# Second MLP projection, columns 1024 to 1535: the moving weights read in another order of columns

## The chip, the cores and the metric

One core of a Trainium2 chip runs the whole program. The metric is device time in microseconds (us). For the kernel before there are three runs: 1775.53, 1778.53 and 1780.2 us, median 1778.53. One further execution was profiled. PE is TensorE, DVE is VectorE, ACT is ScalarE, POOL is GpSimd, and SP issues the large transfers.

## The reference

One layer of a decoder trunk over 256 positions of width 2048. Three branches (gated delta rule, gated linear recurrence, attention into a memory of 256 tokens) are mixed and projected. The part that the change touches is the MLP at the end:

```python
h2 = rmsnorm(x, g_pre_mlp[l])
m = jnp.square(jax.nn.relu(h2 @ w_mlp_in[l])) @ w_mlp_out[l]
x = x + rmsnorm(m, g_post_mlp[l])
```

`w_mlp_in` is 2048 x 8192, `w_mlp_out` 8192 x 2048, all in float32.

## The kernel before, in words

Every large product is done with float32 operands that are split in two: a rounded part (names ending in `h`, made by a cast on ACT) and the rest (names ending in `l`, made by a subtraction on DVE). A product is then three matmuls: activation-high by weight-high, activation-high by weight-low, activation-low by weight-high. The operands have the type `fp32r`, 4 bytes an element. In `T.matmul(out, a, b)` the second argument is the stationary operand, 128 columns that are loaded into the array, and the third is the moving operand, whose columns stream through it. The trace writes the moving operand first: `mm<-oh,mh` moves the weights `oh` over the stationary activation `mh`.

The MLP works in eight steps `e` over the 8192 hidden channels, 1024 at a time. `mlp_in(e)` (lines 1483 to 1513) makes the hidden activation of a step and `mlp_out(e)` (line 1639) adds its share of the second projection. The loop at the end runs `mlp_in(e)` and then `mlp_out(e - 1)`, and `mlp_out_last` does the last step, so `mlp_out` is called for e from 0 to 6. The 2048 output columns are four blocks `c` of 512. Blocks 0 and 1 go through seven block products with sums of weights (`seven`, lines 1542 to 1598), which accumulate in `accs`. Blocks 2 and 3 go straight through `unit` (line 232), with the seven products laid around them: `part(0)` before the unit, `part(1)` in its middle, after its second group of weights.

A call of `unit` here has eight slices of 128 hidden channels, in four groups of two. For each slice and each of the two halves `t` of the positions it issues the three matmuls of lines 256 to 258, each with 512 moving columns: 8 x 2 x 3 = 48 matmuls. They accumulate in two PSUM banks `mm`, one for each half. Behind the unit, one addition for each half on DVE (line 1653) adds the bank to `yacc[c][t]`, 128 x 512 in SBUF; for e = 0 a copy on ACT writes it instead.

The weights of a group come by one DMA from HBM into one of six `raw` buffers (`raw`, line 1452), are cast into `oh` and subtracted into `ol` (`split_w`, line 216), with six pairs of `oh` and `ol` in a ring. A row of `wh[:, j, :]` is 512 elements that lie one behind the other in each partition. PSUM banks named `mm` come from a ring of four (`pbp`) and of two pairs (`pmm`). Nothing in the change alters a queue or the order in which instructions are issued.

Three older steps serve as measures in what follows. Line 1220, on ACT, reads every fourth, every 16th and every 64th element of the tile `bm` (under the name `PP`; its step is 4 x s elements with s = 1, 4, 16) and writes the exponential to `qp`; line 1218 (`seg(0, s)` from `bv(PP, s)`) reads every second element of the same tile when s = 1. Line 475, on DVE, sums the identity matrix `ident`, 128 elements a partition, with a step of 16 elements, into `dblk`. Line 969, also on DVE, sums `tm`, 128 elements that lie one behind the other, into `xc`.

Of the kernel before, what the change touches and what calls it, by code (L numbers as in the profile page):

```python
# [14 lines left out]
ALU = mybir.AluOpType  # L15
# [25 lines left out]
def tile_trunk(ctx: ExitStack, tc, a):  # L41
# [22 lines left out]
    V, A, T = Placed(nc.vector), Placed(nc.scalar), Placed(nc.tensor)  # L64
# [25 lines left out]
    def nm(s):  # L90
        cnt[0] += 1
        return f"{s}_{cnt[0]}"

    def g4(name, shape=(P, 1024), dt=F32):
        return gp.tile(list(shape), dt, tag="g", name=nm(name))
# [11 lines left out]
    def bank(name):  # L107
        return pbp.tile([P, 512], F32, tag="bp", name=nm(name))

    def const(name, shape, dt=F32):  # L110
        return cst.tile(list(shape), dt, tag=name, name=name)
# [76 lines left out]
    def tick(share=1.0):  # L188
        credit[0] += rate[0] * share
        n = int(credit[0])  # L190
        credit[0] -= n
        pump(n)
# [36 lines left out]
    def load_w(src, k0, n, c0, width=512, home=None, aside=False):  # L229
        return split_w(load_w_raw(src, k0, n, c0, width), n, width, home=home, aside=aside)  # L230

    def unit(act, nk, src, c0, r0=0, order=None, split=False, post=None, ws=None, load=None):

        if split:
            ps = [bank("mm") for _ in range(2)]
        else:
            both = pmm.tile([P, 1024], F32, tag="mm", name=nm("mm"))  # L240
            ps = [both[:, 0:512], both[:, 512:1024]]
        if order is None:
            order = [(g, None) for g in range(nk // KG)]
        ws = ws or {}
        for i, (g, tt) in enumerate(order):
            k0 = g * KG
            if g not in ws:
                ws[g] = load(src, r0 + k0, c0) if load else load_w(src, r0 + k0, KG, c0)
            wh, wl = ws[g]
            for j in range(KG):  # L250
                kt = k0 + j
                ah, al = act(kt)
                for t in range(NT) if tt is None else (tt,):
                    o = ps[t]
                    st, sl = ah[:, t * P:(t + 1) * P], al[:, t * P:(t + 1) * P]
                    T.matmul(o, st, wh[:, j, :], start=kt == 0, stop=False)
                    T.matmul(o, st, wl[:, j, :], start=False, stop=False)
                    T.matmul(o, sl, wh[:, j, :], start=False, stop=kt == nk - 1)
            tick()
            if post is not None and i + 1 in post:  # L260
                post[i + 1](ps)
        return ps if split else both
# [34 lines left out]
    def unit_joined(both_of, src, c0):  # L297


        out = g4("sum", (P, 4, S))  # L300
        tiles, ps, ws = [], [], {}
        for i, (gs, h, turned) in enumerate(halved):
            if i in (0, 1):
                tiles.append(pmm.tile([P, 1024], F32, tag="mm", name=nm("mm")))
                ps.extend((tiles[-1][:, 0:512], tiles[-1][:, 512:1024]))
            for g in gs:
                if g not in ws:
                    ws[g] = load_w(src, g * KG, KG, c0, aside=True)
            groups = [(g * KG, ws[g], [flat(both_of(kt)) for kt in range(g * KG, g * KG + KG)]) for g in gs]
            for _ in products_joined(ps, groups, KT, range(4) if h is None else (2 * h, 2 * h + 1), turned):  # L310
                tick(0.5 if h is None else 0.25)
            if 7 in gs:
                o = out[:, 2 * h:2 * h + 2, :]
                p = tiles[h].rearrange("p (c s n) -> p c s n", c=2, s=2)
                A.copy(o, p[:, :, 1, :])
                V.tensor_tensor(out=o, in0=p[:, :, 0, :], in1=o, op=ALU.add)
        return out

    def act_of(tiles):
        return lambda kt: (tiles[kt // 4][0][:, kt % 4, :], tiles[kt // 4][1][:, kt % 4, :])  # L320
# [309 lines left out]
    for u in range(2):  # L630
        ps = unit(mem_act, KT, w_kv, 1024 + 512 * u) if u else first_unit(w_kv, 1024)
        if u == 0:
            bg.append(gen_start())
            pump(1)
        pair = (g4("cvh", (P, NT, 512), F32R), g4("cvl", (P, NT, 512), F32R))
        for t in range(NT):
            split_scaled([(ps[:, t * 512:(t + 1) * 512], pair[0][:, t, :], pair[1][:, t, :], rsm[:, t:t + 1])])
        Vt.append(pair)
# [447 lines left out]
    for hg in range(2):  # L1086
        kc = conv(unit_joined(hboth, w_in, OFF_AK + 512 * hg), 1, hg)
        qc = conv(unit_joined(hboth, w_in, OFF_AQ + 512 * hg), 0, hg)
        vc = conv(unit_joined(hboth, w_in, OFF_AV + 512 * hg), 2, hg)
        z = z_evac(unit(hact, KT, w_in, OFF_AZ + 512 * hg), gna)  # L1090
        bg.append(gen_a(hg, kc, qc, vc, z))
# [213 lines left out]
    for hg in range(2):  # L1305
        k, g = forget(unit_joined(hboth, w_in, OFF_BF + 512 * hg), hg)
        q = unit_joined(hboth, w_in, OFF_BQ + 512 * hg)
        own_table(A.activation(q, q, AF.Silu))
        ps = unit(hact, KT, w_in, OFF_BI + 512 * hg)
# [31 lines left out]
    st = const("sty", [P, 8])  # L1341
# [24 lines left out]
    def mix_last(ps, t):  # L1366
        mix_square(3, t, ps[t])
        v, ry = small("vy", 1), small("ry", 1)
        V.tensor_scalar(out=v, in0=st[:, t * 4 + 3:t * 4 + 4], scalar1=1.0 / D, scalar2=stm[:, t:t + 1],
                        op0=ALU.mult, op1=ALU.add)  # L1370
        G.tensor_tensor(out=ry, in0=v, in1=mhalf[:, 0:1], op=ALU.pow)
        for c in range(4):
            if c == 2:
                mix_gain(3, t, ps[t])
            V.scalar_tensor_tensor(out=xs[c][:, t, :], in0=ys[c][:, t, :], scalar=ry, in1=xs[c][:, t, :],
                                   op0=ALU.mult, op1=ALU.add)
            pt = bank("tr")
            for k in range(4):
                T.transpose(pt[:, k * P:(k + 1) * P], xs[c][:, t, k * P:(k + 1) * P], ident)
            split_scaled([(pt[:, k * P:(k + 1) * P], h2T[c][0][:, k, t * P:(t + 1) * P],  # L1380
                           h2T[c][1][:, k, t * P:(t + 1) * P], gcol[:, 32 + c * 4 + k:33 + c * 4 + k]) for k in range(4)])
# [8 lines left out]
    for c in range(4):  # L1390
        ys.append(g4("y1", (P, NT, 512)))
        if c < 3:
            ps = unit(mact, KT, a["w_out"][0], 512 * c)
# [6 lines left out]
        else:  # L1400
# [3 lines left out]
            ps = unit(mact, KT, a["w_out"][0], 512 * c, order=last, split=True,  # L1404
                      post={8: first_weights, 11: lambda ps: mix_last(ps, 0)})
# [60 lines left out]
    w_mo = a["w_mlp_out"][0]  # L1466
# [142 lines left out]
    yacc = [None] * 4  # L1609
# [25 lines left out]
    def load_xs(c):  # L1635
        xs[c] = g4("x2", (P, NT, 512))
        nc.sync.dma_start(xs[c], xd[c])

    def mlp_out(e, mt, ops, after):
        summed, bare = seven(e, mt, ops)  # L1640
        for c, part in ((2, summed), (3, bare)):
            if c == 3 and after is not None:
                bg.append(after)
            part(0)
            ps = unit(act_of(mt), 8, w_mo, c * 512, e * 8, split=True, load=load_in, post={2: lambda ps: part(1)})
            if e == 0:
                y_ = g4("yacc", (P, NT, 512))
                yacc[c] = [y_[:, t, :] for t in range(NT)]
            for t in range(NT):
                if e == 0:  # L1650
                    A.copy(yacc[c][t], ps[t])
                else:
                    V.tensor_tensor(out=yacc[c][t], in0=ps[t], in1=yacc[c][t], op=ALU.add)

    def mlp_out_last(e, mt):
        yacc[0:2] = joined()
# [23 lines left out]
    for e in range(1, NE):  # L1680
        cur, rs = mlp_in(e)
        drain()
        if e == NE - 1:
            gbc = load_gbc(a["g_post_mlp"])
        later = []
        mlp_out(e - 1, prev, ops, gen_sums(rs, later) if e < NE - 1 else None)
        prev, ops = cur, later
# [15 lines left out]
```

## Time and profile before

| what | value |
|---|---|
| median of three runs | 1778.53 us |
| the profiled execution's own time | 1777.77 us |
| its span, first to last instruction | 1776.0 us |
| mean granted TensorE clock | 0.999 |
| PE busy | 1761.3 us, 99% |
| DVE busy | 1303.4 us, 73% |
| ACT busy | 961.8 us, 54% |
| matmul instructions on the chip | 9053 |
| additions into `yacc` on DVE | 28, mean 688 ns |

The span is 1.8 us shorter than the execution's own time, and the own time 0.8 us below the median. Busy time of matmuls is a union: a matmul's record is longer than the distance to the next one, because they overlap in the array. The rate at which PE works is therefore read from the distance between two starts.

### The profile page before, as it was taken

The page shows a single profiled execution, that of the slowest core. Times are in us where ns is not written, and L with a number is a line of the kernel's source. Part 1 is how long each engine was busy: PE and PEld are TensorE (multiplying, and loading weights), DVE is VectorE, ACT ScalarE, POOL GpSimd, SP SyncE. Part 2 cuts the span into 40 slices and gives each one's busy share as a digit, 9 for nine tenths or more (in the row PEclk, how much of TensorE's full clock was granted, in tenths as well). Part 3 has the DMA queues.
Part 4 walks back from the last instruction along what each step waited for, and adds up shares of the span by engine and source line. Part 5 has one row for each costly group of instructions (what it writes and reads, how often), then busy time and mean ns, then how long its engine had stood idle before and what let it go on. Part 6 is the DMA issues. An engine that isn't in the chain of part 4 may idle for free.

```text
span 1776.0 us, 23962 instructions
## 1 busy us (share of the span) xinstructions
PE 1761.3 (99%) x9053; PEld 1495.8 (84%) x9053; DVE 1303.4 (73%) x1764; ACT 961.8 (54%) x1217; POOL 58.0 (3%) x100
## 2 busy tenths in 40 slices
PE   9999999999999999999999999999999999999998
PEld 7888888888888888888888888888888888888886
DVE  6765768685859487698555557796979797969796
ACT  6644666454555475565444445665545464646453
POOL 1000000400030000000000000000000000000000
PEclk9999999999999999999999999999999999999999
DMA  8665555875587465555666665767767676767683
GB/s 265 214 193 166 168 160 165 220 216 159 161 216 210 135 190 166 158 174 168 188 189 189 235 222 198 233 228 237 229 226 249 220 250 214 257 204 250 212 295 144
DMA packets 188804, 362.84 MB, mean 204 GB/s; under 512 B 14456, under 2 KB 16272, under 8 KB 188304
## 3 DMA queue, kind: packets, MB, share of 16 engines
q1 hardware_dynamic: 181856, 351.32, 62.2%
q0 software_dynamic: 2304, 5.44, 1.5%
q10 hardware_dynamic: 4528, 4.54, 0.9%
q8 instruction: 71, 1.16, 0.3%
q14 instruction: 45, 0.37, 0.1%
HBM read 356.86 MB, written 4.39 MB: 203 GB/s over the span
## 4 chain that ended last, share of the span: by engine, by line
PE 77%; DVE 5%; issue 2%; DMA 1%; ACT 1%; DVEq 0%; POOLq 0%; POOL 0%; ACTq 0%
PE mm L56 73%; DVE ol L56 3%; PE pa L56 1%; DMA raw<-in_w_mlp_out 1%; DVE relu L56 1%; DVE raw L56 1%; PE kk L56 0%; DVE ml L56 0%; PE bo L56 0%; PE o L56 0%; PE pzt L56 0%; PE pw L56 0%; PE tr L56 0%; PE y L56 0%; PE oT L56 0%
## 5 line engine op out<-in xcount | busy, mean ns | idle before, releaser
L56 DVE TENSOR_TENSOR wl<-w,wh 128x1024 fp32r<-128x1024 f32 (+1 forms) x362 | 436.7, 1217 | 234.9 <-ACT wh L56 212.7
L56 ACT CAST wh<-w 128x1024 fp32r<-128x1024 f32 (+1 forms) x362 | 375.5, 1047 | 354.6 <-PE mm L56 293.2
L56 ACT CAST oh<-raw 128x1024 fp32r<-128x1024 f32 x288 | 299.3, 1053 | 274.8 <-PE mm L56 195.8
L56 DVE TENSOR_TENSOR ol<-raw,oh 128x1024 fp32r<-128x1024 f32 x288 | 343.2, 1221 | 95.5 <-ACT oh L56 65.3
L56 PE MATMUL mm<-wh,hh 128*128 128x512 f32 x1152 | 366.2, 392 | 0.0
L56 PEld LDWEIGHTS mm<-wh,hh 128*128 128x128 f32 x1152 | 216.1, 188 | 44.6 <-ACT wh L56 0.3
L56 PE MATMUL mm<-wl,hh 128*128 128x512 f32 x576 | 224.5, 390 | 0.0
L56 PE MATMUL mm<-h2h,oh 128*128 128x512 f32 x960 | 224.3, 390 | 0.0
L56 PEld LDWEIGHTS mm<-h2h,oh 128*128 128x128 f32 x960 | 178.1, 188 | 35.8
L56 PE MATMUL mm<-hh,wh 128*128 128x512 f32 x768 | 184.6, 391 | 0.8 <-ACT z L56 0.8
L56 PEld LDWEIGHTS mm<-hh,wh 128*128 128x128 f32 x768 | 140.6, 188 | 28.3 <-ACT z L56 1.0
L56 PE MATMUL mm<-ol,mh 128*128 128x512 f32 x372 | 145.3, 391 | 1.6 <-DVE ol L56 1.6
L56 PE MATMUL mm<-oh,mh 128*128 128x512 f32 x372 | 145.4, 391 | 0.0
L56 PE MATMUL mm<-oh,ml 128*128 128x512 f32 x372 | 143.8, 389 | 0.0
L56 PEld LDWEIGHTS mm<-wl,hh 128*128 128x128 f32 x576 | 108.2, 188 | 21.2
L56 PEld LDWEIGHTS mm<-h2h,ol 128*128 128x128 f32 x960 | 117.4, 189 | 3.0 <-DVE ol L56 0.7
L56 PE MATMUL mm<-h2h,ol 128*128 128x256 f32 x960 | 118.5, 281 | 0.5 <-DVE ol L56 0.5
L56 PEld LDWEIGHTS mm<-hh,wl 128*128 128x128 f32 x768 | 97.1, 188 | 3.4
L56 PE MATMUL mm<-hh,wl 128*128 128x256 f32 x768 | 99.7, 280 | 0.0
L56 PEld LDWEIGHTS mm<-ol,mh 128*128 128x128 f32 x372 | 69.8, 188 | 17.8 <-DVE ol L56 3.7
L56 PEld LDWEIGHTS mm<-oh,mh 128*128 128x128 f32 x372 | 69.8, 188 | 16.1 <-DVE acc L56 1.6
L56 PEld LDWEIGHTS mm<-oh,ml 128*128 128x128 f32 x372 | 69.8, 188 | 14.4
(363 smaller groups left out, 2208.7 us busy)
## 6 DMA issues: line engine op xcount, KB each, us to landing
w<-in_w_in SPq DMA_DIRECT2D x240, 512.0 KB, 4.2
raw<-in_w_mlp_out SPq DMA_DIRECT2D x170, 512.0 KB, 4.6
raw<-in_w_mlp_in SPq DMA_DIRECT2D x118, 512.0 KB, 4.8
w<-in_w_out SPq DMA_DIRECT2D x32, 512.0 KB, 4.2
w<-in_w_kv_mem SPq DMA_DIRECT2D x30, 512.0 KB, 5.0
w<-in_w_br_c SPq DMA_DIRECT2D x16, 512.0 KB, 3.6
w<-in_w_br_a SPq DMA_DIRECT2D x16, 512.0 KB, 4.3
w<-in_w_br_b SPq DMA_DIRECT2D x16, 512.0 KB, 3.6
```

What stands on the lines that cost most here:

```text
L56: ins = op(*args, **kwargs)
```

## The change

A table `turns` gives each `e` a pair (b, q). In block 2 the 512 columns of a slice of weights are seen as b runs, in each of which the elements are read with a step of q: first the elements 0, q, 2q and so on of the run, then 1, q + 1 and so on. All three matmuls of a slice read their moving operand that way. The columns of the two PSUM banks then stand in this other order, and the addition into `yacc` writes (and reads) `yacc` with the same pattern, which puts them right. The bank itself is read straight through. For e = 0 the pair is (1, 1), and for block 3 too: nothing changes there.

| e | (b, q) | step between elements read one after the other | elements in one sweep |
|---|---|---|---|
| 1 | (1, 2) | 2 elements, 8 bytes | 256 |
| 2 | (1, 16) | 16 elements, 64 bytes | 32 |
| 3 | (1, 64) | 64 elements, 256 bytes | 8 |
| 4 | (32, 2) | 2 elements, 8 bytes | 8, in runs of 16 |
| 5 | (1, 4) | 4 elements, 16 bytes | 128 |
| 6 | (8, 4) | 4 elements, 16 bytes | 16, in runs of 64 |

```diff
-    def unit(act, nk, src, c0, r0=0, order=None, split=False, post=None, ws=None, load=None):
+    def unit(act, nk, src, c0, r0=0, order=None, split=False, post=None, ws=None, load=None, way=lambda x_: x_):
...
-                    T.matmul(o, st, wh[:, j, :], start=kt == 0, stop=False)
-                    T.matmul(o, st, wl[:, j, :], start=False, stop=False)
-                    T.matmul(o, sl, wh[:, j, :], start=False, stop=kt == nk - 1)
+                    T.matmul(o, st, way(wh[:, j, :]), start=kt == 0, stop=False)
+                    T.matmul(o, st, way(wl[:, j, :]), start=False, stop=False)
+                    T.matmul(o, sl, way(wh[:, j, :]), start=False, stop=kt == nk - 1)
...
+    turns = [(1, 1), (1, 2), (1, 16), (1, 64), (32, 2), (1, 4), (8, 4)]
+
     def mlp_out(e, mt, ops, after):
...
-            ps = unit(act_of(mt), 8, w_mo, c * 512, e * 8, split=True, load=load_in, post={2: lambda ps: part(1)})
+            b, q = turns[e] if c == 2 else (1, 1)
+            ps = unit(act_of(mt), 8, w_mo, c * 512, e * 8, split=True, load=load_in, post={2: lambda ps: part(1)},
+                      way=lambda x_: x_.rearrange("p (b a q) -> p b q a", b=b, q=q))
...
-                    V.tensor_tensor(out=yacc[c][t], in0=ps[t], in1=yacc[c][t], op=ALU.add)
+                    y_ = yacc[c][t].rearrange("p (b a q) -> p b q a", b=b, q=q)
+                    V.tensor_tensor(out=y_, in0=ps[t].rearrange("p (b q a) -> p b q a", b=b, q=q), in1=y_, op=ALU.add)
```

Every engine has as many instructions as before, in the same places. The only rows that read otherwise are the twelve additions of the six slices on DVE. Here they are for e = 2, with their neighbours:

```order
 L56 TENSOR_TENSOR ol_9710<-raw_9703,oh_9709 128x1024
 L56 TENSOR_TENSOR relu_11187<-relu_11187 128x4x128
-L56 TENSOR_TENSOR yacc_10422<-mm_11566,yacc_10422 128x512
-L56 TENSOR_TENSOR yacc_10422<-mm_11567,yacc_10422 128x512
+L56 TENSOR_TENSOR yacc_10422<-mm_11566,yacc_10422 128x16x32
+L56 TENSOR_TENSOR yacc_10422<-mm_11567,yacc_10422 128x16x32
 L56 TENSOR_TENSOR ol_9712<-raw_1690_9704,oh_9711 128x1024
 L56 TENSOR_TENSOR relu_11187<-relu_11187,relu_11355 128x4x128
```

The addition has the same 512 elements in 16 sweeps of 32; nothing stands elsewhere than before.

## The prediction

> **What bounds the kernel now.** I read the page's table of busy time first, then the waits of PE, then the sequence in time around one of the changed slices.
>
> ```profile
> PE 1761.3 (99%) x9053; PEld 1495.8 (84%) x9053; DVE 1303.4 (73%) x1764; ACT 961.8 (54%) x1217; POOL 58.0 (3%) x100
> PE mm L56 <- DVE ol L56: 3.2, 7, 1.1
> PE mm L56 <- DVE ol L56: 1.6, 5, 0.6
> ```
>
> The second row is from PE's waits over the whole span, the third from the same view for 1250 to 1700 us, where the first five changed slices lie. PE is busy for all but 14.7 us of the span, and in that stretch it waits five times for a subtraction on DVE, 1.6 us together. So whatever lengthens or shortens a matmul there moves the end by as much, except for those 1.6 us.
>
> The next rows are PE's sequence of instructions in time, for e = 1: start, duration, engine, line, operation.
>
> ```profile
> 1267.21 0.39 PE L56 MATMUL mm<-oh,mh 128*128 128x512 f32 x1
> 1268.22 0.50 PE L56 MATMUL mm<-ol,mh 128*128 128x512 f32 x1 [0.62 <-DVE ol L56]
> ...
> 1270.31 0.39 PE L56 MATMUL mm<-oh,mh 128*128 128x512 f32 x1
> ...
> 1275.52 0.39 PE L56 MATMUL mm<-oh,ml 128*128 128x512 f32 x1
> ```
>
> From 1270.31 to 1275.52 lie 23 distances of the second half of the changed unit (24 of its 48 matmuls): 5.21 / 23 = 0.2266 us for 512 moving columns. That is the rate, not the 0.39 of a record. The wait at 1268.22 stands between the unit's halves, in the seven products.
>
> Does the distance follow the columns? In the first projection two runs of 32 stand behind each other, one of 256 and one of 512 columns:
>
> ```profile
> 1310.26 3.93 PE L56 MATMUL mm<-h2h,ol 128*128 128x256 f32 x32
> 1314.02 7.44 PE L56 MATMUL mm<-h2h,oh 128*128 128x512 f32 x32
> 1321.30 0.87 PE L56 MATMUL mm<-h2h,ol 128*128 128x256 f32 x6
> ```
>
> 3.76 / 32 = 0.1175 us and 7.28 / 32 = 0.2275 us: 256 more columns cost 0.110 us, 0.43 ns a column. PE is bound by its columns, nearly without a fixed part.
>
> **The change: the matmuls.** It removes and adds no instruction and moves none. Six slices of 48 matmuls, 288 in all, read their moving operand with a step. Two slices (e = 1 and 4, 96 matmuls) take every second element, 8 bytes apart; four (e = 2, 3, 5, 6, 192 matmuls) take elements 16, 64 or 256 bytes apart. No matmul of the trace does that, so the price is bounded from other engines that read SBUF with a step. These are groups of ACT and of DVE by shape:
>
> ```profile
> L56 ACT ACTIVATE kp<-bR 128x1024 f32<-128x1024 f32 x4 | 4.2, 1058 | 0.4 <-DVE bR L56 0.3
> L56 ACT ACTIVATE junk<-x 128x512 f32<-128x512 f32 x16 | 9.9, 620 | 0.0
> L56 ACT ACTIVATE qp<-bm 128x256 f32<-128x256 f32 x2 | 1.3, 658 | 0.0
> L56 ACT ACTIVATE qp<-bm 128x64 f32<-128x64 f32 x2 | 0.6, 309 | 0.0
> ...
> L56 DVE TENSOR_REDUCE ss<-sq 128x8 f32<-128x1024 f32 x4 | 4.9, 1221 | 4.2 <-ACT sq L56 4.2
> L56 DVE TENSOR_REDUCE xc<-tm 128x8 f32<-128x128 f32 x4 | 1.2, 289 | 0.1
> L56 DVE TENSOR_REDUCE dblk<-ident 128x16 f32<-128x128 f32 x1 | 0.4, 368 | 0.0
> ```
>
> On ACT, elements that lie one behind the other cost (1058 - 620) / 512 = 0.855 ns each, which leaves 182 ns fixed. The 256 elements of `qp<-bm` lie 16 bytes apart, the 64 elements 64 bytes: (658 - 309) / 192 = 1.82 ns each, and (309 - 182) / 64 = 1.98 ns for the 64 alone. Hence 256 elements with a step take longer than 512 without. On DVE, neighbours cost (1221 - 289) / 896 = 1.04 ns, and `dblk<-ident`, 64 bytes apart, takes 79 ns longer than `xc<-tm` for as many elements: 1.04 + 79 / 128 = 1.66 ns. Since a step of 64 bytes costs about what one of 16 does, the unit paid for is a piece of 16 bytes, 1.66 to 1.98 ns each, whatever is used of it.
>
> What of a step of 8 bytes, two elements a piece? The first exponentials over `bm` are one of 512 elements with that step and one of 256 with a step of 16 bytes; the view of the tile's instructions, for 649 to 651 us and for 651 to 656 us, where only the latter is left:
>
> ```profile
> L56 ACT ACTIVATE qp<-bm x2: 665/667/669, 650.0 to 650.5; 128x512 f32<-128x512 f32 x1, 128x256 f32<-128x256 f32 x1
> L56 ACT ACTIVATE qp<-bm x1: 665/665/665, 650.5 to 650.5; 128x256 f32<-128x256 f32 x1
> ```
>
> So 669 ns for 512 elements in 256 pieces: (669 - 182) / 256 = 1.90 ns a piece, again the same. ACT hardly feels it, because two elements cost it 1.71 ns anyway.
>
> Now PE. Its 512 columns without a step are 128 pieces of 16 bytes in 226.6 ns: 1.77 ns a piece. That is just the price of a piece on the other two engines, between DVE's 1.66 and ACT's 1.98. I take this as PE's limit too: PE already gets its moving operand as fast as pieces come, four columns to a piece. Then a step of 8 bytes needs 256 pieces, 453 ns (+226.6), and a step of 16 bytes or more 512 pieces, 906 ns (+680).
>
> The bounds: at the low end nothing (the row of 226.6 ns, if PE fetches ahead of need); a gain is excluded, since columns, bytes and instructions are the same. At the high end ACT's dearest rows: 512 x 1.98 - 226.6 = 787 ns and 256 x 1.90 - 226.6 = 260 ns. I take 1.77 ns, as it is PE's own row and the nearest to both measures.
>
> Sum: 96 x 0.2266 = 21.8 us and 192 x 0.680 = 130.5 us, together 152.3 us; by the high end 25 + 151 = 176 us, by 1.72 ns a piece (four times the 0.43 ns a column) 21 + 127 = 148 us.
>
> [...]
>
> **The additions and the waits.** Twelve additions of `yacc` on DVE read one operand and write with the step; the eight with 16 bytes or more may be slower.
>
> ```profile
> L56 DVE TENSOR_TENSOR yacc<-mm,yacc 128x512 f32<-128x512 f32 x28 | 18.6, 688 | 6.0 <-PE mm L56 5.7
> ...
> 1262.00:1280.00 18.00, 17.38 (x75) 13.65 (x75) 17.98 (x20) 11.34 (x12) 0.00 (x0) 1.00 0.82 264
> 1258.87:1264.32 5.45, 5.45 (x26) 4.50 (x25) 5.45 (x6) 3.06 (x3) 0.00 (x0) 1.00 0.57 183
> ```
>
> The windows give length, then busy time of PE, weight loads, DVE and ACT. An addition takes 688 ns; with DVE's 0.62 ns more an element the read adds 0.32 us, and as much again if the write pays too: 0.64 us, 8 x 0.64 = 5.1 us. DVE is full from 1262 to 1280 (17.98 of 18.00), so without cover this could reach PE through the next `ol`. But in my case the cover grows: half a unit with a long step takes 24 x 0.906 = 21.7 us in place of 5.45, and DVE's work in it stays what it was. I cost the additions at nothing, and the five waits at -1.6 us, because DVE, which they are for, gets ahead during the longer unit. Transfers and casts likewise have more time; what is late next is PE itself.
>
> The end: the profiled execution took 1777.8 us (span 1776.0 and 1.8 around it), 0.8 below the median. 1777.8 + 152.3 - 1.6 = 1928.5. I say 1928; this case's own range is 148 - 1.6 to 176 - 1.6 above, 1924 to 1952.
>
> **The rivals.** *Two elements a piece are enough* (PE fetches pieces twice as fast as ACT does): 8-byte steps are free, the others halve the rate. For it: engines of different speed could have ports of different speed, and PE's 1.77 ns is only an upper bound of what a piece costs it. Against: the three prices agree within 20%. 192 x 0.2266 = 43.5, less 1.6: 1820. [...]
>
> *Any step halves the rate* (two neighbours are fetched together, otherwise one): 288 x 0.2266 = 65.3, less 1.6: 1841. For it: nothing but that 8 bytes is what two columns need. Against: 64 and 16 bytes would have to cost what 8 do, while on ACT the piece of 16 bytes decides.
>
> *Not slower: PE's reads are fetched far enough ahead.* Place: the read of the moving operand, all 288 matmuls. It decides if PE can get a new piece for every column, one each 0.43 ns, four times as fast as 1.77. Then the distance stays 0.2266, the matmuls cost nothing, and only the additions remain, 0 to 5.1 us against waits of 1.6: 1777 to 1783. For it: the trace never shows PE waiting for an operand in SBUF, and 0.43 ns a column may simply be the array's own rate. Against: ACT and DVE both pay although their columns come two to three times slower.
>
> That the change does not do what it says is no case: the additions have the new pattern, and the matmuls must have it for the sums to meet.
>
> **How the numbers follow.** My case 0.50; two a piece 0.20; any step 0.07; not slower 0.18; something else 0.05 (mixtures of steps and runs, or above 1952). A measurement here tells about 0.3%, 5.3 us, from no change. "Not slower" reaches to +5 us, so 0.03 of its 0.18 goes to slower and 0.14 to the same, 0.01 to faster. Slower: 0.50 + 0.20 + 0.07 + 0.05 + 0.03 = 0.85. The range takes in my case, any step and two a piece, from a little below 1820 (a rate halved from a slightly faster one, 192 x 0.2 = 38 less 1.6: 1814) to 1952 rounded: 1813 to 1950. It leaves out "not slower" and the tails, about 0.2.
>
> **What would show it.** Right: the distance between starts in the unit of block 2 is about 0.45 us for e = 1 and 4 and 0.9 us for e = 2, 3, 5, 6, alike for all three matmuls of a slice; block 3's units stay at 0.227; PE's waits for `ol` in 1250 to 1700 us are gone; DVE is no longer full there. Two a piece: 0.227 for e = 1 and 4. Any step: 0.45 in all six. Not slower: 0.227 everywhere. Wrong in another way: a price that grows with the step (e = 3 above e = 5), that depends on the run (e = 4 unlike e = 1, e = 6 unlike e = 5), or a granted clock that falls while PE streams slowly.

## The result, and the profile after

| | before | after |
|---|---|---|
| median of the runs | 1778.42 us | 1841.70 us (1840.77 to 1843.23, 4 runs) |
| span of the profiled execution | 1776.0 us | 1840.1 us |
| mean granted TensorE clock | 0.999 | 0.999 |

The ratio is 1.0357, with a 95% interval of 1.0344 to 1.0370. The change costs 63.3 us. Forecast were 149.5: the sign was right, the size more than twice too large. The time is inside the range, and within 1 us of the rival "any step halves the rate", so the first question is whether that rival's reason is the right one. (It is not.)

The page's busy times and PE's waits over the whole span:

```profile
PE 1826.8 (99%) x9053; PEld 1502.1 (82%) x9053; DVE 1307.2 (71%) x1764; ACT 961.9 (52%) x1217; POOL 57.8 (3%) x100
PE mm L56 <- DVE ol L56: 1.4, 2, 0.9
```

PE's busy time has grown by 65.5 us, the span by 64.1. Both remaining waits for `ol` lie outside the changed stretch: between 1250 and 1760 us the view of PE's waits is empty. The window that was full on DVE before now reads (length, then busy time of PE, weight loads, DVE, ACT):

```profile
1262.00:1280.00 18.00, 18.00 (x53) 10.27 (x52) 13.53 (x14) 7.17 (x7) 0.00 (x0) 1.00 0.63 203
```

PE is full, DVE has fallen from 17.98 to 13.53. The price itself stands in PE's sequence in time. These are the first and the last start of the 24 matmuls in the second half of the changed unit, for e = 1 to 6 in order:

```profile
1274.86 0.61 PE L56 MATMUL mm<-oh,mh 128*128 128x512 f32 x1
1285.27 0.63 PE L56 MATMUL mm<-oh,ml 128*128 128x512 f32 x1
...
1370.38 0.59 PE L56 MATMUL mm<-oh,mh 128*128 128x512 f32 x1
1380.33 0.61 PE L56 MATMUL mm<-oh,ml 128*128 128x512 f32 x1
...
1466.80 0.72 PE L56 MATMUL mm<-oh,mh 128*128 128x512 f32 x1
1478.06 0.67 PE L56 MATMUL mm<-oh,ml 128*128 128x512 f32 x1
...
1564.44 0.64 PE L56 MATMUL mm<-oh,mh 128*128 128x512 f32 x1
1575.46 0.66 PE L56 MATMUL mm<-oh,ml 128*128 128x512 f32 x1
...
1661.32 0.62 PE L56 MATMUL mm<-oh,mh 128*128 128x512 f32 x1
1671.88 0.64 PE L56 MATMUL mm<-oh,ml 128*128 128x512 f32 x1
...
1757.71 0.62 PE L56 MATMUL mm<-oh,mh 128*128 128x512 f32 x1
1768.27 0.64 PE L56 MATMUL mm<-oh,ml 128*128 128x512 f32 x1
```

Each difference, divided by 23, is the distance between two matmuls:

| e | step | distance, us | against 0.2266 |
|---|---|---|---|
| 1 | 8 bytes | 0.4526 | 2.00 |
| 2 | 64 bytes | 0.4326 | 1.91 |
| 3 | 256 bytes | 0.4896 | 2.16 |
| 4 | 8 bytes, runs of 16 elements | 0.4791 | 2.11 |
| 5 | 16 bytes | 0.4591 | 2.03 |
| 6 | 16 bytes, runs of 64 elements | 0.4591 | 2.03 |

The six excesses over 0.2266 add up to 1.4125 us; times 48 that is 67.8 us. PE's busy time, which holds no waits, has grown by 65.5; less the 1.6 us of waits that are gone the sum is 66.2, against 64.1 in the span. So the rate of the 288 matmuls accounts for the whole cost, to within some 2 us. Step for step: 8 bytes cost what was forecast; 16 bytes and more cost a third of what was forecast.

### The profile page after: what moved, and what is told of

Same layout as the page of the kernel before. It is cut to its first block, busy times and chain, and to the rows that moved or that the text cites. A ratio compares the mean times of both kernels' runs of the same rounds, so it can differ in the third digit from the quotient of the medians.

```text
span 1840.1 us, 23962 instructions
## 1 busy us (share of the span) xinstructions
PE 1826.8 (99%) x9053; PEld 1502.1 (82%) x9053; DVE 1307.2 (71%) x1764; ACT 961.9 (52%) x1217; POOL 57.8 (3%) x100
## 4 chain that ended last, share of the span: by engine, by line
PE 83%; DVE 1%; ACT 1%; issue 1%; DMA 0%; DVEq 0%; POOLq 0%; POOL 0%
PE mm L56 79%; PE pa L56 1%; PE kk L56 0%; DVE ol L56 0%; PE bo L56 0%; PE o L56 0%; ACT oh L56 0%; DMA raw<-in_w_mlp_out 0%; PE pzt L56 0%; PE pw L56 0%; PE tr L56 0%; DVE raw L56 0%; PE y L56 0%; PE oT L56 0%; PE mgT L56 0%
## 5 line engine op out<-in xcount | busy, mean ns | idle before, releaser
L56 PE MATMUL mm<-oh,mh 128*128 128x512 f32 x372 | 169.8, 456 | 0.0
L56 PE MATMUL mm<-ol,mh 128*128 128x512 f32 x372 | 169.1, 455 | 0.0
L56 PE MATMUL mm<-oh,ml 128*128 128x512 f32 x372 | 168.1, 455 | 0.0
```

The lines of the kernel that those rows point to most:

```text
L56: ins = op(*args, **kwargs)
```

## The experiments

After the result my own account (one piece of 16 bytes each 1.77 ns, whatever is used of it) could not stand as it was: four times as many pieces cost only twice the time (433 to 490 ns for 512, 226.6 for 128). What remained were three theories. PAIR: PE takes two columns at once where they are neighbours, otherwise one (the reason behind the rival that met the time). PIECE: a piece of 16 bytes costs a fixed time, but about half of what I took. ROW: the fast rate needs one unbroken run. Most kernels change only block 2 in the six slices, so that one execution gives six prices, each read from PE's sequence as above. The third leaves the matmuls straight, and the fourth and the last two go beyond block 2.

### Runs of neighbours kept together

```diff
-    turns = [(1, 1), (1, 2), (1, 16), (1, 64), (32, 2), (1, 4), (8, 4)]
+    turns = [(1, 1), (2, 2), (8, 2), (32, 2), (2, 4), (4, 4), (2, 16)]
...
-                      way=lambda x_: x_.rearrange("p (b a q) -> p b q a", b=b, q=q))
+                      way=lambda x_: x_.rearrange("p (a q r) -> p q a r", q=q, r=r))
```

> Six slices as in the change, but short runs of neighbours stay together: pairs of elements 16, 64 and 256 bytes apart (e = 1, 2, 3), four elements every 32 and every 64 bytes (e = 4, 5), sixteen every 128 bytes (e = 6). Theory PAIR (PE takes two columns at once where they are neighbours in 8 bytes, else one, so that any single-element step doubles a matmul): the distance between matmuls stays at 0.217 to 0.227 us in all six, time 1775 to 1782 us. Theory PIECE (a 16-byte piece costs 0.85 to 1.77 ns, the prediction's idea in a milder form): 0.45 us for e = 1 to 3, 0.227 for e = 4 to 6, 1778 + 144 x 0.226 = 1811 us. Theory ROW (the fast rate needs one run over all 512 columns): 0.45 us in all six, about 1843 us.

Measured: 1807.54 us, ratio 1.0176 (1.0160 to 1.0193). Pairs 16 and 64 bytes apart, then four neighbours every 64 bytes, first and last of 24 starts:

```profile
1273.46 0.61 PE L56 MATMUL mm<-oh,mh 128*128 128x512 f32 x1
1283.87 0.63 PE L56 MATMUL mm<-oh,ml 128*128 128x512 f32 x1
...
1368.98 0.59 PE L56 MATMUL mm<-oh,mh 128*128 128x512 f32 x1
1378.89 0.61 PE L56 MATMUL mm<-oh,ml 128*128 128x512 f32 x1
...
1643.52 0.39 PE L56 MATMUL mm<-oh,mh 128*128 128x512 f32 x1
1648.68 0.38 PE L56 MATMUL mm<-oh,ml 128*128 128x512 f32 x1
```

0.4526, 0.4309 and 0.2243 us. The pairs 256 bytes apart took 0.4896, the four neighbours every 32 bytes 0.2313, sixteen every 128 bytes 0.240. PAIR and ROW fall. The numbers are PIECE's, but a pair costs what a single element costs at the same step, to within 1.5% (at 16 bytes 0.4526 for two columns a piece and 0.4591 for one, at 256 bytes 0.4896 for both), and that PIECE cannot say.

The view of `yacc` shows the additions of this kernel, which go in pairs or longer runs (shortest, median and longest in ns; in the changed kernel the longest took 1119):

```profile
L56 DVE TENSOR_TENSOR yacc<-mm,yacc x28: 681/692/693, 1283.2 to 1797.6; 128x512 f32<-128x512 f32 x28
```

### Other single steps

```diff
-    turns = [(1, 1), (1, 2), (1, 16), (1, 64), (32, 2), (1, 4), (8, 4)]
+    turns = [(1, 1), (8, 4), (1, 2), (1, 4), (1, 8), (1, 32), (1, 128)]
```

> Single elements again, other patterns in other slices: e = 1 runs of 64 with a step of 4, e = 2 a step of 2, e = 3 of 4, e = 4 of 8, e = 5 of 32, e = 6 of 128. If the pattern decides and not the slice, the distances of the changed kernel come back where they now stand: 0.460 us at e = 1, 0.453 at e = 2, 0.460 at e = 3. Theory PAIR: all six within 0.427 to 0.50 us, and the differences between patterns come from something smaller. A price that grows with the step in bytes would make e = 6 the dearest; a price for each sweep (1.1 ns, from 16 sweeps at 0.433 and 64 at 0.487 us) gives about 0.425, 0.451 and 0.56 us for e = 4, 5, 6.

Measured: 1829.77 us in one run (1776.12 for the kernel before on that chip). The patterns that moved kept their price: 0.4591, 0.4526 and 0.4596 us. Steps of 8 and 32 took 0.4300 and 0.4335, so neither bytes nor the count of sweeps set the price. The last expectation missed altogether: a step of 128, with sweeps of four elements, took 0.28 us.

### The additions alone

```diff
-                      way=lambda x_: x_.rearrange("p (b a q) -> p b q a", b=b, q=q))
+                      way=lambda x_: x_)
```

> The additions alone: the matmuls read their weights straight, the twelve additions keep the pattern, so columns 1024 to 1535 come out in a wrong order. The prediction costs the additions at nothing beside the longer units, at 0 to 5.1 us without that cover. The changed kernel's trace has the eight additions at 1.04 to 1.12 us instead of 0.69, 3.2 us in all. Off the path: ratio 1.000 within 0.001. On the path: 1.002.

Measured: 1776.08 us, ratio 1.0001 (0.9992 to 1.0010). The view of the tile `yacc` of this kernel:

```profile
L56 DVE TENSOR_TENSOR yacc<-mm,yacc x28: 681/692/1107, 1274.2 to 1765.7; 128x512 f32<-128x512 f32 x28
```

The additions do get longer, to 1.1 us instead of 0.69. PE waits for none of them; ACT does once, 0.4 us. They cost nothing that can be measured (less than 1.8 us, by the interval) even without the cover of the longer units.

### Neighbours off a boundary

```diff
-        return pairs[-1][0], shifted(pairs[-1][1], 16 if aside else 0)
+        return pairs[-1][0], shifted(pairs[-1][1], 16 if aside else 1)
```

> The kernel before, with the low weights of the second projection one element (4 bytes) further on in their buffers, so that they still lie one behind the other but start off an 8-byte boundary; high weights as before. Theory PAIR with fixed pairs (8-byte boundaries): neighbours 0 and 1 lie in different pairs; either the matmuls that move ol take 0.45 us like those with a step, which adds 484 x 0.226 = 109 us, or PE fetches ahead and only one fetch in 512 is added, 0.227 us and no change. PAIR with free pairs: 0.227 us.

Measured: 1782.43 us in one run, against 1776.12. Over the last 213 matmuls of the second projection the mean distance between starts is 0.2333 us, where the kernel before has 0.2267. That is 0.02 us for each group of three, one of which moves `ol`; the starts, given to 0.01 us, do not show in which of the three it lies. For all 1452 matmuls 0.0066 us each makes 9.6 us, of which 6.3 arrive; PE's waits for `ol` fall from 3.2 to 1.1 us, which is 2.1 of the rest. Neither 0.45 nor quite nothing. The start is no cause of the doubling.

### Very short sweeps

```diff
-    turns = [(1, 1), (1, 2), (1, 16), (1, 64), (32, 2), (1, 4), (8, 4)]
+    turns = [(1, 1), (64, 2), (32, 4), (8, 16), (2, 64), (1, 256), (128, 2)]
```

> Very short sweeps of single elements, because a step of 128 with sweeps of four took 0.28 us where all other single steps take 0.43 to 0.49. e = 1 four elements 8 bytes apart within runs of 8; e = 2 four 16 bytes apart within 16; e = 3 four 64 bytes apart within 64; e = 4 four 256 bytes apart within 256; e = 5 two elements 1024 bytes apart; e = 6 neighbours in the order 0, 2, 1, 3 within each 16 bytes. Theory COUNT (sweeps of four, or of fewer, are taken together whatever the step): 0.28 us for e = 1 to 4. Theory REUSE (the few pieces of 16 bytes read last are kept, so the next sweep over the same pieces is free): 0.28 or less in all six. Theory FAR (elements 512 bytes or more apart are read side by side): 0.43 to 0.49 for e = 1 to 4 and e = 6, 0.28 or less for e = 5. Were only whole neighbour runs fast: 0.43 to 0.5 in all six.

Measured: 1785.18 us in one run, against 1777.52. First and last of 24 starts for e = 1 and for e = 5:

```profile
1270.50 0.50 PE L56 MATMUL mm<-oh,mh 128*128 128x512 f32 x1
1278.31 0.51 PE L56 MATMUL mm<-oh,ml 128*128 128x512 f32 x1
...
1621.80 0.38 PE L56 MATMUL mm<-oh,mh 128*128 128x512 f32 x1
1626.76 0.38 PE L56 MATMUL mm<-oh,ml 128*128 128x512 f32 x1
```

0.3396 and 0.2157 us; e = 2, 3 and 4 took 0.2683, 0.2691 and 0.2817, and e = 6 took 0.2265. No theory had all of it. The surprise is e = 5: columns 0, 256, 1, 257 and so on, not two of them neighbours, go *faster* than a straight row (0.2266).

### Four neighbours further apart

```diff
-    turns = [(1, 1), (2, 2), (8, 2), (32, 2), (2, 4), (4, 4), (2, 16)]
+    turns = [(1, 1), (8, 4), (16, 4), (32, 4), (64, 4), (64, 2), (128, 2)]
```

> Runs of four neighbours (16 bytes) further apart: 128, 256, 512 and 1024 bytes (e = 1 to 4); pairs in sweeps of four and two, 512 and 1024 bytes apart (e = 5, 6). Theory that a whole piece of 16 bytes always goes at the full rate: 0.224 to 0.24 us for e = 1 to 4; if the price falls with the step as from 32 bytes (0.231) to 64 bytes (0.224), it may reach 0.217, below the 0.2268 of neighbours, which would be worth using in all slices. Pairs: FAR and COUNT give 0.28 or less for e = 5, FAR also for e = 6; otherwise 0.43 to 0.49 as for the other pairs.

Measured: 1795.43 us in one run, against 1777.52. Four neighbours 128, 256, 512 and 1024 bytes apart: 0.2457, 0.2783, 0.2678, 0.2504 us, so the hoped-for 0.217 is not there and whole pieces further apart are dearer by up to 23%. Pairs in sweeps of four: 0.4443; in sweeps of two: 0.3391. Far apart is not fast by itself.

### Two sides

One idea says most of this. It is my estimate, fitted to the distances so far; no trace shows its parts. Suppose that PE took its moving columns in two streams, the even and the odd ones, and that each side paid 1.77 ns (226.6 / 128) for every new piece of 16 bytes, the piece that the rows of ACT and DVE gave. To keep up, a side would then have to find two of its own columns in each piece. A straight row would give each side exactly two and be just at the limit (0.2266 us). Any single step would give one, pairs too (a pair would split between the sides): 256 new pieces a side, 256 x 1.77 = 453 ns, where singles took 430 to 490 and pairs 431 to 490. And two runs read in turn would give four, so that pieces would no longer bound the row (0.2157 us).

```diff
+    turns = [("b a q", "b q a", 1, 1), ("a b h q", "h b q a", 64, 2), ("b a q", "b q a", 2, 128), ("b a q", "b q a", 8, 32),
+             ("b a q", "b q a", 64, 4), ("b a q", "b q a", 16, 16), ("b a q", "b q a", 4, 64)]
...
+                        T.matmul(o_, st, h_, start=kt == 0 and o_ is os[0], stop=False)
+                        T.matmul(o_, st, l_, start=False, stop=False)
+                        T.matmul(o_, sl, h_, start=False, stop=kt == nk - 1 and o_ is os[-1])
...
+                      way=lambda x_: (lambda v: [v[:, 0], v[:, 1]] if "h" in f else [v])(x_.rearrange(f"p ({f}) -> p {g}", **n)))
```

> Theory LANES: the even and the odd columns of the stream are fetched apart, each side keeps one piece of 16 bytes, a new piece costs it 1.7 to 1.8 ns, and so it needs two columns from each piece to keep up. Then neighbours just keep up (two columns a side from each piece, 0.2268), pairs and single steps have one column a side from each piece (0.43 to 0.49), and two runs taken in turn have four (0.2155). e = 1: two runs 1024 bytes apart taken in turn, but only two neighbours of each piece and then the next piece, the other two in a second matmul of 256 columns: like the pairs each piece gives two columns at a time, but both on one side. LANES says as fast as neighbours, 0.113 to 0.12 us for 256 columns; if a piece must simply give four columns in a row, 0.22. e = 2 to 6: two runs taken in turn, 512, 128, 16, 64 and 256 bytes apart: LANES 0.2155 in all (e = 4, with 16 bytes: pieces taken in turn, four columns a side); if only far runs are read side by side, the near ones 0.43 or more.

Measured: 1778.70 us in one run, against 1775.88. First and last of the 48 starts of 256 columns for e = 1, and of the 24 for e = 4:

```profile
1269.33 0.28 PE L56 MATMUL mm<-oh,mh 128*128 128x256 f32 x1
1274.96 0.28 PE L56 MATMUL mm<-oh,ml 128*128 128x256 f32 x1
...
1526.74 0.38 PE L56 MATMUL mm<-oh,mh 128*128 128x512 f32 x1
1531.70 0.38 PE L56 MATMUL mm<-oh,ml 128*128 128x512 f32 x1
```

5.63 / 47 = 0.1198 us for 256 columns, close to the 0.1175 of neighbours in the first projection, and 0.2157 us; the other four took 0.2157 to 0.2161. All six are as LANES had them, down to runs 16 bytes apart. The first is the one that tells it apart: two columns from each piece, as with the pairs (0.4526 us for 512 columns), but by the idea both on the same side, and the doubling is gone. One reader that pays 1.77 ns a piece would need 128 x 1.77 = 227 ns there. This order was measured at one distance only, 1024 bytes between the runs. The kernel as a whole is not faster than the one before: in this execution PE waits 5.3 us for `ol` and `acc`, where it waited 3.2 us for `ol`.

### The order that is faster, in the whole second projection

```diff
+    def turned(x_):
+        return x_.rearrange("p (a q) -> p q a", a=2)
...
-            T.matmul(ps[i], ah, wh[:, j, :], start=begin, stop=False)
+            T.matmul(ps[i], ah, turned(wh[:, j, :]), start=begin, stop=False)
...
-            ps = unit(act_of(mt), 8, w_mo, c * 512, e * 8, split=True, load=load_in, post={2: lambda ps: part(1)})
+            ps = unit(act_of(mt), 8, w_mo, c * 512, e * 8, split=True, load=load_in, post={2: lambda ps: part(1)}, way=turned)
...
-            V.scalar_tensor_tensor(out=x_, in0=y_, scalar=rs, in1=x_, op0=ALU.mult, op1=ALU.add)
+            V.scalar_tensor_tensor(out=straight(x_), in0=y_, scalar=rs, in1=straight(x_), op0=ALU.mult, op1=ALU.add)
```

> The order that took 0.2155 us in one slice, columns 0, 256, 1, 257 and so on, for all 1452 matmuls of the second projection that move weights (864 in the units of all eight steps, 588 in the seven products). Sums and products stay in that order and are put right where the last gain and the last addition read them. If the price holds for all: 1452 x (0.2268 - 0.2155) = 16.4 us, time 1761 us, ratio 0.991. If DVE, full around the seven products, takes it back by its waits: up to half, about 1769 us. If 0.2155 was peculiar to one slice: no change.

Measured: 1766.34 us, ratio 0.9950 (0.9937 to 0.9964). Its slices run at 0.2155 to 0.2161 us each, so the price holds everywhere; 9.5 us of the 16.4 arrive. PE's busy time falls by 15.2 us, and its waits come back.

```profile
PE mm L56 <- DVE ol L56: 4.5, 7, 1.3
...
PE mm L56 <- DVE acc L56: 1.4, 2, 1.2
```

That is 5.9 us of waiting for DVE where there were 3.2, and so 2.7 of the 6.9 us that are missing; the rest stays open.

### And in the first projection and the joined input projections

```diff
-                            T.matmul(ps[c], wh[:, j, c * P:(c + 1) * P], both[j], start=k0 + j == 0, stop=end)
+                            T.matmul(ps[c], wh[:, j, c * P:(c + 1) * P], both[j].rearrange("p (s a q) -> p s q a", s=2, a=2), start=k0 + j == 0, stop=end)
...
-                    A.copy(r[:, c, :], ps[c][:, S:2 * S])
-                    V.tensor_tensor(out=r[:, c, :], in0=ps[c][:, 0:S], in1=r[:, c, :], op=ALU.add)
+                    o = r[:, c, :].rearrange("p (a q) -> p a q", a=2)
+                    p = ps[c].rearrange("p (s q a) -> p s a q", s=2, a=2)
+                    A.copy(o, p[:, 1])
+                    V.tensor_tensor(out=o, in0=p[:, 0], in1=o, op=ALU.add)
```

> As e7_two, and besides the first MLP projection and the joined input projections, where the activations move: each half of 256 positions is read 0, 128, 1, 129 and so on (960 + 896 matmuls of 512 columns, as many of 256), and the copy and the addition that follow read PSUM with a step of 8 bytes and write straight. LANES: 1856 x (0.2275 - 0.2159) = 21.5 us from the wide ones and, if the narrow ones fall from 0.1175 to 0.109 as columns at 0.4217 ns would have it, 15 us more; with the 9.5 us of e7_two about 1730 us, ratio 0.974, less what waits for DVE take back. If the side by side reading does not hold for these operands, or the copies from PSUM become the bound: 1766 us or above.

Measured: 1745.63 us, ratio 0.9828 (0.9815 to 0.9842), faster than both kernels. PE's sequence in time, runs of 32 merged, and PE's longest waits:

```profile
1288.80 3.73 PE L56 MATMUL mm<-h2h,ol 128*128 128x256 f32 x32
1292.38 7.07 PE L56 MATMUL mm<-h2h,oh 128*128 128x512 f32 x32
1299.28 0.94 PE L56 MATMUL mm<-h2h,ol 128*128 128x256 f32 x7
```

```profile
PE mm L56 <- DVE ol L56: 8.8, 13, 1.7
PE mm L56 <- DVE relu L56: 2.8, 5, 1.0
```

6.90 / 32 = 0.2156 us for 512 columns, 3.58 / 32 = 0.1119 for 256 (0.2275 and 0.1175 before). The 256 fell less than the 0.109 expected, and the waits for DVE rose to 11.6 us in these two rows alone, so DVE is the first place to look for the next gain. 30.4 us is what remains, against 46 expected.

## Why the prediction was half right

**What bounds the kernel** was right: PE without slack, nearly every added nanosecond of the 288 matmuls in the end. The span grew by 64.1 us, the sum of the measured distances less the waits is 66.2. (The 23 distances that the prediction takes from 1270.31 on begin three matmuls early, in the seven products; from 1270.99 on, in the unit itself, the rate is the same 0.2266.)

**The waits and the additions** were right. The five waits between 1250 and 1700 us are gone, and the additions, up to 1.1 us long, cost nothing that can be measured; alone they give a ratio of 1.0001, so the 5.1 us that I kept as an upper end was not needed. (Less the waits, that rival's sum is 1776 to 1781, not 1777 to 1783.)

**The steps of 8 bytes** were right as a number: 226.6 ns more forecast, 226 and 252.5 measured; 23.0 us for the two slices against 21.8. That they met it is luck as far as the reason goes: 256 pieces one after the other and, by the idea of two sides, 256 on each side come to the same 453 ns.

**The steps of 16 bytes and more** are the step of the sum that failed: "a step of 16 bytes or more 512 pieces, 906 ns (+680)". Measured are 432.6 to 489.6 ns, +206 to +263. The term was 130.5 us and is 44.8. What failed is the count of pieces, one after the other for all columns: 512 pieces took about as long as 256 (433 to 490 ns against 453 and 479), and 128 pieces in the order of two runs in turn took 119.8 ns, not 227. The price of a piece need not be at fault. By the idea of two sides 1.77 ns, read off the straight row, would still give 453 ns: 256 a side would be the most there can be, and a step of 8 bytes would already reach it. I took the agreement of three prices (1.66, 1.77 and 1.98 ns) for a proof that PE pays its pieces one after the other, although PE takes a column in 0.43 ns where ACT takes 0.855 and DVE 1.04. That two readers are the reason is argued, not shown. Two signs that the prediction named for being wrong also came, each small: e = 3 is 7% above e = 5, and e = 4 is 6% above e = 1. The first is no price that grows with the step, since 32 and 128 bytes took 0.4300 and 0.4335.

**The rival that met the time**, "any step halves the rate", met it for a wrong reason. "Two neighbours are fetched together, otherwise one" is refuted by pairs, which cost as much as single elements (0.4526), and by 0, 256, 1, 257, which is faster than the row. Its 1841 us were met because all six patterns do come out near twice the rate; by the idea of two sides, because each of them would need a new piece for every column of a side.

**The rival "two elements a piece are enough"** fell at e = 1 and 4 (0.4526 and 0.4791 us, where it has 0.227), and again with the pairs, which have two columns in a piece and double the time (0.4526 at 16 bytes). It fits better if the two are counted for every other column, though even then four neighbours 256 bytes apart took 0.2783. On DVE two a piece were enough: additions that go in pairs took 0.69 us, single elements 8 bytes apart 0.69 too, the single ones 16 bytes apart 1.1. On ACT they cost 8% more: 669 ns for 512 elements 8 bytes apart, 620 for 512 neighbours.

## What to carry to other kernels

Cost a strided moving operand by an order that was measured. In sweeps of eight columns or more, single columns 8 to 256 bytes apart and pairs every 16 to 512 bytes took a 512-column `fp32r` matmul here from 0.227 to between 0.43 and 0.49 us; four neighbours every 32 to 1024 bytes took 0.224 to 0.278. A price read from another engine's rows (1.66 to 1.98 ns a piece) did not say how the count of pieces adds up on PE, where 512 took 433 to 490 ns and not 906; before such a price is multiplied up, ask for a row that shows the count. And a straight row need not be the floor: two runs read in turn took 0.2157 us against 0.2266, 5% more rate.

## What the runs showed of the hardware

- A straight row of 512 `fp32r` columns is not PE's fastest order here: 0.2266 us, against 0.2155 to 0.2161 for two runs in turn, at run distances from 16 to 1024 bytes.
- In the last kernel, reading PSUM with a step of 8 bytes did not lengthen the ACT copies (378 ns against 373) nor the DVE additions (416 against 416).
- Open: why single steps differ by 14% (0.4300 us at 32 bytes, 0.4896 at 256); why four neighbours cost 0.2243 at 64 bytes and 0.2783 at 256, where the idea of two sides says 0.2266 for both; why very short sweeps cost less (0.3391 for pairs in sweeps of two, 0.268 to 0.282 for single columns in sweeps of four from 16 bytes apart on, where the idea of two sides says 0.453). That idea fits most of the prices and foretold six of them, but nothing here shows the two readers themselves, nor that PE pays by 16 bytes.
